# A transformer layer on one core: last filter weights on 128 rows, modulation tiles spread over four groups, first normalised inputs read from PSUM

## The chip, the core and the metric

The kernel runs on one core of a Trainium2 chip. TensorE (PE) multiplies; VectorE (DVE) and ScalarE (ACT) do the elementwise work; SyncE (SP) has a queue of its own from which it issues DMA transfers. Each engine works through its instructions in order. The metric is the device time of one execution in microseconds (us), and the median of several runs is compared.

## The reference

One layer of a backbone over 256 latent tokens with 256 context tokens, D = 1024, in float32. Every sub-layer is normalised and modulated by numbers that come from `c` (latent) or `c_ctx` (context) through one large matrix `w_ada`:

```
mod = silu(c) @ w_ada + b_ada            # 9 x 1024 numbers; the same for c_ctx
h   = rmsnorm(s, g_pre) * (1 + scale) + shift
ffn: s + 0.5 * gate * rmsnorm((silu(h @ w_gate) * (h @ w_up)) @ w_out, g_post)   # d_ff 2816
```

The layer is FFN 1, then token mixers (a long convolution and a differential attention), then FFN 2. The filter of the long convolution is made by a small MLP over 256 positions:

```
h = sin(freq * (z @ w1 + b1)); h = sin(freq * (h @ w2 + b2)); h = sin(freq * (h @ w3 + b3))
h = h @ w4                               # 256 x 64 by 64 x 2048
k = [h_fwd * decay, h_bwd * decay reversed] / (sum |k| + eps)
```

## The kernel before

**Numbers in two parts.** Matmuls have to keep float32 accuracy, so each operand is split into a high part, rounded to the type float32r, and the rest. `split` does it: ACT copies the high part, DVE subtracts. Three matmuls (`mm3`: high by high, high by low, low by high) make one product.

**Weights.** All weights of the layer come in units of 128 x 1024 (or 128 x 896) in a fixed list `plan`. `W()` hands out the next unit and has `prefetch` load and split later ones: four buffers `raw`, three of `wh` and `wl`. SP issues the loads, ACT makes `wh`, DVE makes `wl`, PE multiplies.

**FFN 1** is cut into groups over d_ff, `GROUPS1 = [(0, 7), (7, 14), (14, 22)]` in tiles of 128. Each group has a c loop, in which `ffn_in` takes two weight units and 48 matmuls (`ffi`) per tile c and `ffn_act` makes the activation `sg` and its parts `ah` and `al`, and a d loop over 8 output tiles, in which `ffn1_out` takes one unit and 3 matmuls (`ffo`) for each tile c of the group, 21 in the first two groups. These two groups work on all 512 columns (256 latent, 256 context). The third group runs twice, first on the 256 latent columns ("group 2" in the table below), then on the 256 context columns ("group 3"). The first three c of group 0 are done in the prologue, over quarters of the model's width, since the first modulation numbers arrive by quarters (`ada_quarter`, `ada_row`, `ada_cols`); so its c loop begins with c = 3. The prologue's instructions stand in program order; after it, `InOrder.pin = False` lets a scheduler choose the order on each engine.

**Modulation numbers.** The other 56 tiles of `w_ada` (128 x 1024, 512 KB each) are loaded by `ada(i)` into two buffers `adaw`, and DVE multiplies a tile by the broadcast `silu(c)` and sums it along the row (`junk`, a reduction). The first 24 tiles are needed for the context as well and take two reductions each, the others one. These reductions keep their order in the program. A table says how many tiles `some_ada` issues behind each c and each d of a group:

```
ADA = [([0] * 6 + [2], [1] * 8), ([3] * 5 + [4] * 2, [2] * 8), ([1] * 8, [0] * 8), ([0] * 8, [0] * 8)]
```

**The filter MLP** is a generator, `filters()`, which FFN 1 pumps forward between its own matmuls. Its last layer has `h3` on 128 rows (high part of the hidden values in rows 0 to 63, low part in 64 to 127) and the weights `fw4` loaded twice, in both halves of the rows. Two matmuls make a product `fo`: `h3` by `w4h` on 128 rows, and the high half of `h3` by `w4l` on 64. Eight such products are made, two at each of four places.

**The first normalised inputs.** In the prologue `tok_bcast` leaves 1/rms of each token, spread over all partitions, in a PSUM tile `bc`; ACT copies it to `rb`, and `normed(q)` multiplies two k tiles of the latent and of the context input by it on DVE, to give `xr`; `ada_cols` makes `hh` and `hl` of them.

Of the kernel before, what the change touches and what calls it, by code (L numbers as in the profile page):

```python
# [35 lines left out]
WARM, WARM2, WARM3, WARM4 = 9, 2, 5, 10  # L36
NF, NF1 = 4, 2

ADA = [([0] * 6 + [2], [1] * 8), ([3] * 5 + [4] * 2, [2] * 8), ([1] * 8, [0] * 8), ([0] * 8, [0] * 8)]


V_C, V_CC, V_NG, V_BA, V_CW, V_CB, V_HB, V_SG = 0, 8, 16, 64, 136, 208, 232, 240
# [23 lines left out]
def tile_layer(ctx: ExitStack, tc: tile.TileContext, A: dict, out: bass.AP):  # L66
# [14 lines left out]
    def G(name, dt=F32):  # L81
        return gp.tile([P, 512], dt, tag="g", bufs=NG, name=name)

    def T(name, dt=F32):
        return gp.tile([P, 512], dt, tag="t", bufs=NT, name=name)
# [133 lines left out]
    def split(src, hi, lo):  # L219
        act.activation(hi, src, AF.Copy)  # L220
        dve.tensor_tensor(lo, src, hi.bitcast(F32), ALU.subtract)
# [64 lines left out]
    def tok_bcast(y, n):  # L286

        bc = ps("bc")
        for i in range(n):
            pe.matmul(bc[:, i * P:(i + 1) * P], lhsT=y[:, i:i + 1].to_broadcast([P, P]), rhs=ident,  # L290
                             start=True, stop=True)
        return bc[:, :n * P]
# [122 lines left out]
    def filters():  # L415
        fz = T("fz")
        nc.sync.dma_start(fz[0:64, 0:448], A["fzw"])
        hcur = fz[0:64, 0:SEQ]
        fw4 = [G("fw4") for _ in range(4)]
        decay = [G("decay") for _ in range(4)]  # L420
        fh, fl = Arr("fh", 4, P, F32R), Arr("fl", 4, P, F32R)
        for i in (0, 2, 1, 3):
            for r in range(2):
                nc.sync.dma_start(fw4[i][64 * r:64 * r + 64, :], A["fw4"][:, i * 512:(i + 1) * 512])
        for i in (0, 2, 1, 3):
            nc.sync.dma_start(decay[i], A["decay"][:, i // 2, (i % 2) * 512:(i % 2) * 512 + 512])
        fraw = T("fraw")
        nc.sync.dma_start(fraw, A["dft"])
        for i in range(3):
            o = ps("fmlp")[0:64, 0:SEQ]  # L430
            pe.matmul(o, lhsT=fz[0:64, SEQ + 64 * i:SEQ + 64 * i + 64], rhs=hcur, start=True, stop=True)
            hn = T("fhid")[0:64, 0:SEQ]
            fsin(hn, o, i)
            hcur = hn
            yield

        h3 = T("h3", F32R)[:, 0:SEQ]
        act.activation(h3[0:64, :], hcur, AF.Copy)
        dve.tensor_tensor(h3[64:P, :], hcur, h3[0:64, :].bitcast(F32), ALU.subtract)
        w4 = [(G("w4h", F32R), G("w4l", F32R)[0:64, :]) for _ in range(4)]  # L440
        for i in (0, 2, 1, 3):
            act.activation(w4[i][0], fw4[i], AF.Copy)
            dve.tensor_tensor(w4[i][1], fw4[i][0:64, :], w4[i][0][0:64, :].bitcast(F32), ALU.subtract)
        yield
        yield
        for k in range(4):
            fh.at(k), fl.at(k)
        split(fraw, fh.tiles[0], fl.tiles[0])
        nrm = ps("nrm")
        pds, abl = [], []  # L450
        for cb in range(2):
            pd = []
            for tt in range(2):
                hf, hb = T("hf"), T("hb")
                for z, dst in ((0, hf), (1, hb)):
                    o = ps("fo")
                    r = slice(tt * P, (tt + 1) * P)
                    pe.matmul(o, lhsT=h3[:, r], rhs=w4[2 * z + cb][0], start=True, stop=False)
                    pe.matmul(o, lhsT=h3[0:64, r], rhs=w4[2 * z + cb][1], start=False, stop=True)
                    mk = vec[:, V_MASK:V_MASK + 1] if (z == 1 and tt == 0) else 1.0  # L460
                    dve.scalar_tensor_tensor(dst, o, mk, decay[2 * tt + cb], ALU.mult, ALU.mult)
                parts = []
                for op in (ALU.add, ALU.subtract):
                    v = T("pd")
                    dve.tensor_tensor(v, hf, hb, op)
                    vh, vl = G("ph", F32R), G("pl", F32R)
                    split(v, vh, vl)
                    parts.append((vh, vl))
                pd.append(parts)
                act.activation(hf, hf, AF.Abs)  # L470
                act.activation(hb, hb, AF.Abs)
                if tt == 0:
                    ab = T("ab")
                    dve.tensor_tensor(ab, hf, hb, ALU.add)
                else:
                    dve.tensor_tensor(ab, ab, hf, ALU.add)
                    dve.tensor_tensor(ab, ab, hb, ALU.add)
                yield
            yield
            for w in range(2):  # L480
                eo = [ps("kf") for _ in range(2)]
                for tt in range(2):
                    mm3(eo[tt], fh.at(2 * w + tt), fl.at(2 * w + tt), pd[tt][w][0], pd[tt][w][1], True, True)
                for slot, v in butterfly(w, eo, "kev"):
                    nc.sync.dma_start(kdram[:, cb, slot, :], v)
                yield
                yield
            for j in range(4):
                pe.matmul(nrm[:, cb * 4 + j:cb * 4 + j + 1], lhsT=ab[:, j * P:(j + 1) * P], rhs=ones[:, 0:1],
                          start=True, stop=True)  # L490
        dve.tensor_scalar(rn, nrm[:, 0:8], EPS, None, ALU.add)
        dve.reciprocal(rn, rn)
# [23 lines left out]
    def ada_row(q):  # L516
        n = 4
        row = T("row")
        act.activation(row[0:n, :], arow[q][0:n, :], AF.Copy)
        arow[q] = row[0:n, :]  # L520
# [18 lines left out]
        for k in range(n):  # L539
            pe.matmul(arow[q][0:4, :], lhsT=c4[:, k, :], rhs=araw[q, k], start=k == 0, stop=False)  # L540

    def normed(q):
        for k in (2 * q, 2 * q + 1):
            xr[k] = T("xr")
            dve.tensor_tensor(xr[k][:, 0:SEQ], xs[:, k, :], rb[:, 0:SEQ], ALU.mult)
            dve.tensor_tensor(xr[k][:, SEQ:T2], cs.at(k), rb[:, SEQ:T2], ALU.mult)

    def ada_cols(q):
        acol = ps("acol")
        for j in range(4):  # L550
            pe.matmul(acol[:, 2 * j:2 * j + 2], lhsT=arow[q][:, j * P:(j + 1) * P], rhs=sel[0:arow[q].shape[0], :],
                      start=True, stop=True)
        av = acol[:, 0:8].rearrange("p (i k r) -> p r i k", i=2, k=2)
        k0 = 2 * q
        m01 = modall[:, :, 0:16].rearrange("p r (i k) -> p r i k", i=2)[:, :, :, k0:k0 + 2]
        b01 = vec[:, V_BA:V_BA + 16].rearrange("p (i k) -> p i k", i=2)[:, :, k0:k0 + 2]
        g0 = vec[:, V_NG + k0:V_NG + k0 + 2]
        for r in range(2):
            dve.tensor_tensor(m01[:, r], av[:, r], b01, ALU.add)
        for r in range(2):  # L560
            dve.scalar_tensor_tensor(gsall[:, r, k0:k0 + 2], m01[:, r, 1], 1.0, g0, ALU.add, ALU.mult)
        for k in (k0, k0 + 1):
            for r in range(2):
                t = slice(r * SEQ, (r + 1) * SEQ)
                sh, gs = modall[:, r, k:k + 1], gsall[:, r, k:k + 1]
                if k == k0 and r == 1:
                    dve.tensor_scalar(hh[:, k, t], xr[k][:, t], gs, sh, ALU.mult, ALU.add)
                else:
                    act.activation(hh[:, k, t], xr[k][:, t], AF.Identity, bias=sh, scale=gs)
            for r in range(2):  # L570
                t = slice(r * SEQ, (r + 1) * SEQ)
                sh, gs = modall[:, r, k:k + 1], gsall[:, r, k:k + 1]
                dve.tensor_scalar(xr[k][:, t], xr[k][:, t], gs, sh, ALU.mult, ALU.add)
            dve.tensor_tensor(hl[:, k, :], xr[k], hh[:, k, :].bitcast(F32), ALU.subtract)
# [5 lines left out]
    for k in range(1, NF):  # L580
        pe.matmul(arow[0][0:4, :], lhsT=c4[:, k, :], rhs=araw[0, k], start=False, stop=False)
    ada_split(0, NF)
    rb = T("rb")
    act.activation(rb, tok_bcast(y, 4), AF.Copy)
    ada_quarter(0, NF)
    normed(0)
    prefetch(1, 3)
    keep_warm(WARM3)
    ada_row(0)
    ada_cols(0)  # L590
    ada_raw(1, NF1)
    pg = [ps("ffi") for _ in range(2 * NE)]
    acts = []
    for q in range(4):
        w = W("early", q, 0, ahead=2)
        if q < 3:
            ada_split(q + 1, NF1 if q == 0 else 0)
        if q < 2:
            ada_load(q + 2)
        n = 4 if q == 0 else 3  # L600
        quarter(q, pg[0:n], w, T2)
        w2 = W("early", q, 1, ahead=2)
        if q < 3:
            ada_quarter(q + 1, NF1 if q == 0 else 0)
            ada_row(q + 1)
            normed(q + 1)
        if n == 3:
            quarter(q, pg[3:4], w, T2, 3)
        else:
            quarter(q, pg[4:5], w2, T2)  # L610
        if q < 3:
            ada_cols(q + 1)
        quarter(q, pg[n + 1:], w2, T2, n - 3)
# [657 lines left out]
```

## Time and profile before

| what | value |
|---|---|
| median of three runs | 997.32 us (994.62, 997.32, 999.21) |
| profiled execution, its time | 996.32 us |
| its span on the core | 994.6 us |
| mean granted clock of PE | 0.994 of full |
| busy: PE, DVE, ACT | 978.8, 772.9, 491.2 us |
| bytes moved | 183.04 MB, mean 184 GB/s |

The profile shows one execution. "Busy" is the time in which an engine had an instruction under way. The steps between the starts of matmuls tell more than their durations, since matmuls overlap. Nearly all instructions are recorded under line 59, because a helper issues them, so they are told apart by the names of their tiles (`fo`, `ffo`, `wl`, `junk` and so on). The prologue with the first three c lasts until about 60 us, group 0 until about 165, group 1 until about 286, and the two halves of the last group run behind it, the latent one first.

### The profile page before, as it was taken

To read this page: it belongs to the slowest core of one execution; us is meant where nothing else is said; L and a number is where in the kernel's file an instruction comes from. 1 tells how busy PE (TensorE), PEld (TensorE's weight loads), DVE (VectorE), ACT (ScalarE), POOL (GpSimd) and SP (SyncE) were. 2 spreads that over 40 slices of the span, in tenths; PEclk is the share of its full clock that TensorE was granted. 3 is DMA by queue.
4 is the path that set the end of the run, shared out by engine and by line. 5 is a ranking of instruction groups with operands and counts; after the bars stand their busy time and mean duration, and the time that the engine had idled before them with its cause. 6 is when DMAs were issued, how large, how long until landed. Compare 5 with 4: busy or idle time off the path is not lost.

```text
span 994.6 us, 16285 instructions
## 1 busy us (share of the span) xinstructions
PE 978.8 (98%) x6250; PEld 873.0 (88%) x6250; DVE 772.9 (78%) x1471; ACT 491.2 (49%) x811; POOL 0.2 (0%) x4
## 2 busy tenths in 40 slices
PE   9999999999989999999999999999999999999996
PEld 6677787888779999999988899898899899999995
DVE  6886788998778778789877977867978777666666
ACT  6553434222124545566564445755675465444443
POOL 0000000000000000000000000000000000000000
PEclk9999999999989999999999999999999999999998
DMA  9845274677889755555653245444445546656661
GB/s 316 304 133 169 72 255 150 232 230 242 266 267 321 251 180 174 169 188 164 217 180 106 86 160 154 144 148 128 132 130 180 163 157 195 185 180 188 189 190 64
DMA packets 63525, 183.04 MB, mean 184 GB/s; under 512 B 6792, under 2 KB 15576, under 8 KB 63448
## 3 DMA queue, kind: packets, MB, share of 16 engines
q1 hardware_dynamic: 60856, 177.80, 56.2%
q10 hardware_dynamic: 2592, 4.20, 1.6%
q8 instruction: 49, 0.80, 0.3%
q14 instruction: 28, 0.23, 0.1%
HBM read 174.63 MB, written 3.15 MB: 179 GB/s over the span
## 4 chain that ended last, share of the span: by engine, by line
PE 81%; DMA 8%; DVE 7%; ACT 2%; issue 2%; SPq 1%; DVEq 0%; ACTq 0%
PE ffi L59 29%; PE ffo L59 8%; PE ho L59 6%; DMA adaw<-in_wadaT_dram 6%; PE pk L59 4%; PE px L59 4%; PE pva L59 3%; DVE junk L59 3%; PE pq L59 2%; PE pgd L59 2%; PE yhy L59 2%; PE pv L59 2%; PE pgh L59 2%; PE yda L59 2%; PE yo L59 2%; PE arow L59 2%
## 5 line engine op out<-in xcount | busy, mean ns | idle before, releaser
L59 ACT ACTIVATE wh<-raw 128x1024 fp32r<-128x1024 f32 (+1 forms) x250 | 259.1, 1040 | 335.5 <-issue 126.9
L59 DVE TENSOR_TENSOR wl<-raw,wh 128x1024 fp32r<-128x1024 f32 (+1 forms) x250 | 298.2, 1195 | 74.0 <-ACT wh L59 72.0
L59 PE MATMUL ffi<-hh,wl 128*128 128x258 f32 (+2 forms) x832 | 259.6, 314 | 3.8 <-DVE wl L59 3.8
L59 PE MATMUL ffi<-hh,wh 128*128 128x258 f32 (+2 forms) x832 | 260.7, 315 | 0.0
L59 PE MATMUL ffi<-hl,wh 128*128 128x258 f32 (+2 forms) x832 | 248.2, 313 | 0.0
L59 PEld LDWEIGHTS ffi<-hh,wl 128*128 128x128 f32 x832 | 160.0, 192 | 13.1 <-DVE wl L59 4.3
L59 PEld LDWEIGHTS ffi<-hh,wh 128*128 128x128 f32 x832 | 160.1, 192 | 11.7 <-issue 1.4
L59 PEld LDWEIGHTS ffi<-hl,wh 128*128 128x128 f32 x832 | 157.3, 192 | 9.0
L59 DVE CUSTOM_DVE_ANT_0 junk<-adaw,cb 128x1024 f32<-128x1024 f32 x80 | 97.7, 1221 | 26.3 <-DMA adaw<-in_wadaT_dram 25.4
L59 PE MATMUL ho<-wh,a 128*128 128x512 f32 x176 | 55.9, 390 | 0.0
L59 PE MATMUL ffo<-a,wh 128*128 128x256 f32 x256 | 46.8, 284 | 0.1
L59 PE MATMUL ffo<-al,wh 128*128 128x512 f32 x112 | 43.7, 390 | 0.4 <-DVE al L59 0.4
L59 PE MATMUL ffo<-ah,wh 128*128 128x512 f32 x112 | 43.9, 392 | 0.0
L59 PE MATMUL ffo<-ah,wl 128*128 128x512 f32 x112 | 43.6, 389 | 0.0
L59 PEld LDWEIGHTS ffo<-a,wh 128*128 128x128 f32 x256 | 40.0, 192 | 0.5 <-DVE a L59 0.5
L59 PEld LDWEIGHTS ho<-wh,a 128*128 128x128 f32 x176 | 33.1, 188 | 6.6
L59 PE MATMUL px<-hh,wh 128*128 128x256 f32 x128 | 36.2, 283 | 0.0
L59 PE MATMUL px<-hl,wh 128*128 128x256 f32 x128 | 36.2, 283 | 0.0
L59 PE MATMUL px<-hh,wl 128*128 128x256 f32 x128 | 36.2, 283 | 0.0
L59 PE MATMUL ffo<-a,wl 128*128 128x256 f32 x128 | 36.2, 283 | 0.0
L59 PE MATMUL ho<-wl,a 128*128 128x512 f32 x88 | 34.4, 390 | 0.0
L59 ACT ACTIVATE e<-sc,sm 128x512 f32<-128x512 f32 x32 | 21.8, 685 | 11.4 <-DVE sm L59 4.1
(312 smaller groups left out, 1979.6 us busy)
## 6 DMA issues: line engine op xcount, KB each, us to landing
raw<-in_wi_dram SPq DMA_DIRECT2D x100, 512.0 KB, 3.6
adaw<-in_wadaT_dram SPq DMA_DIRECT2D x56, 512.0 KB, 4.4
raw<-in_win_dram SPq DMA_DIRECT2D x56, 512.0 KB, 3.6
raw<-in_wo_dram SPq DMA_DIRECT2D x38, 512.0 KB, 3.6
araw<-in_wada_dram SPq DMA_DIRECT2D x32, 256.0 KB, 6.2
raw<-in_wo_dram SPq DMA_DIRECT2D x16, 448.0 KB, 3.7
raw<-in_winv_dram SPq DMA_DIRECT2D x8, 512.0 KB, 4.4
raw<-in_whyo_dram SPq DMA_DIRECT2D x8, 512.0 KB, 3.5
```

Of the source, the lines that this page charges most:

```text
L59: r = op(*args, **kwargs)
```

## The change

Three edits. (a) `w4l` is made on all 128 rows and multiplied with all of `h3`, so that the product of the two low parts is added as well. (b) The table `ADA`: the c loop of group 0 issues 7 tiles (2, 2, 1, 2 behind c = 3 to 6) instead of 2, the d loop of group 1 issues 8 instead of 16, the d loop of group 2 stays at none and its c loop at one per c, and two tiles stand behind the first two c of group 3. Tiles issued by the end of group 0: 15 instead of 10; of group 1: 46 instead of 49; of group 2: 54 instead of 56. (c) The first call of `normed` reads `bc` in PSUM; the copy `rb` comes behind `ada_row(0)`, and later calls read `rb`.

```
-ADA = [([0] * 6 + [2], [1] * 8), ([3] * 5 + [4] * 2, [2] * 8), ([1] * 8, [0] * 8), ([0] * 8, [0] * 8)]
+ADA = [([0] * 3 + [2, 2, 1, 2], [1] * 8), ([3] * 5 + [4] * 2, [1] * 8), ([1] * 8, [0] * 8), ([1] * 2 + [0] * 6, [0] * 8)]
...
-        w4 = [(G("w4h", F32R), G("w4l", F32R)[0:64, :]) for _ in range(4)]
+        w4 = [(G("w4h", F32R), G("w4l", F32R)) for _ in range(4)]
         for i in (0, 2, 1, 3):
-            act.activation(w4[i][0], fw4[i], AF.Copy)
-            dve.tensor_tensor(w4[i][1], fw4[i][0:64, :], w4[i][0][0:64, :].bitcast(F32), ALU.subtract)
+            split(fw4[i], *w4[i])
...
-                    pe.matmul(o, lhsT=h3[0:64, r], rhs=w4[2 * z + cb][1], start=False, stop=True)
+                    pe.matmul(o, lhsT=h3[:, r], rhs=w4[2 * z + cb][1], start=False, stop=True)
...
-    def normed(q):
+    def normed(q, rb):
...
-    rb = T("rb")
-    act.activation(rb, tok_bcast(y, 4), AF.Copy)
+    bc = tok_bcast(y, 4)
     ada_quarter(0, NF)
-    normed(0)
+    normed(0, bc)
     prefetch(1, 3)
     keep_warm(WARM3)
     ada_row(0)
+    rb = T("rb")
+    act.activation(rb, bc, AF.Copy)
...
-            normed(q + 1)
+            normed(q + 1, rb)
```

How the instructions move on an engine is seen in the order of each kernel. On DVE, in group 0's c loop, at the third sine of the filter MLP (`fa` and `fk` are its steps; `ISA junk` is a reduction, `ISA modall` its result's read-out):

```order
 L59 TENSOR_SCALAR fa<-fa 64x256
+L59 ISA junk,modall<-adaw,cb_150 128x1024
+L59 ISA modall 128x1
+L59 ISA junk,modall<-adaw,cb_151 128x1024
+L59 ISA modall 128x1
 L59 TENSOR_SCALAR fa<-fmlp,vec 64x256
-L59 TENSOR_TENSOR wl<-raw,wh 128x1024
+L59 ISA junk,modall<-adaw,cb_150 128x1024
+L59 ISA modall 128x1
 L59 TENSOR_SCALAR fk<-fa 64x256
```

Reductions that stood behind group 0's last `al` now stand among the steps of the sine; before, only a `wl` stood there. On PE, in group 0's d loop of the changed kernel, 17 `ffo` matmuls behind the loop's first (`kf` are matmuls of the filter's transform, which read the parts `ph` and `pl`):

```order
+L59 MATMUL ffo<-ah,wl 128x512
+L59 MATMUL kf<-ph,fh 128x512
+L59 MATMUL kf<-pl,fh 128x512
+L59 MATMUL kf<-ph,fl 128x512
+L59 MATMUL kf<-ph,fh 128x512
+L59 MATMUL ffo<-ah,wh 128x512
+L59 MATMUL ffo<-al,wh 128x512
+L59 MATMUL ffo<-ah,wl 128x512
+L59 MATMUL kf<-pl,fh 128x512
+L59 MATMUL kf<-ph,fl 128x512
+L59 MATMUL ffo<-ah,wh 128x512
```

The scheduler has spread these matmuls: in the kernel before, the six `kf` stood together behind the 21st `ffo`. Nine `ffo` stand between the last of these `kf` and the first matmul that reads the `al` of c = 6. On DVE, in group 1's d loop (`hsb` adds an output tile to what group 0 left):

```order
 L59 TENSOR_TENSOR hsb<-ffo,hsb 128x512
-L59 TENSOR_TENSOR wl<-raw,wh 128x896
-L59 ISA junk,modall<-adaw,cb_150 128x1024
-L59 ISA modall 128x1
-L59 ISA junk,modall<-adaw,cb_150 128x1024
-L59 ISA modall 128x1
+L59 ISA junk,modall<-adaw,cb_150 128x1024
+L59 ISA modall 128x1
+L59 TENSOR_TENSOR wl<-raw,wh 128x896
 L59 TENSOR_TENSOR hsb<-ffo,hsb 128x512
```

Between two output tiles there are two reductions before and one in the changed kernel, and the `wl` of a unit to come has changed places with the reduction beside it.

## Rows read from the trace of the kernel before

**Rows 1.** Page, part 1: busy us of each engine (share) and its instructions.

```profile
PE 978.8 (98%) x6250; PEld 873.0 (88%) x6250; DVE 772.9 (78%) x1471; ACT 491.2 (49%) x811; POOL 0.2 (0%) x4
```

**Rows 2.** Chain of waits near 295: start us, us, engine, what.

```profile
287.48 4.99 DMA adaw<-in_wadaT_dram
...
292.61 1.23 DVE junk L59
293.84 0.60 DVE hsb L59
294.44 1.14 DVE wl L59
...
295.63 4.38 PE ffi L59 x22
```

**Rows 3.** Stretches: length, busy PE, PEld, DVE, ACT, POOL; PEclk, DMA share, GB/s.

```profile
87.40:121.80 34.40, 34.40 (x144) 26.42 (x144) 25.30 (x40) 17.59 (x28) 0.00 (x0) 1.00 0.24 68
165.00:282.00 117.00, 116.56 (x518) 96.24 (x517) 97.03 (x146) 31.71 (x39) 0.00 (x0) 1.00 0.75 240
284.00:300.00 16.00, 12.16 (x73) 11.74 (x73) 11.89 (x18) 3.12 (x4) 0.00 (x0) 0.79 0.83 272
300.00:316.00 16.00, 16.00 (x135) 15.94 (x134) 14.31 (x30) 7.88 (x12) 0.00 (x0) 1.00 0.89 314
365.00:400.00 35.00, 35.00 (x295) 35.00 (x294) 28.92 (x57) 18.06 (x32) 0.00 (x0) 1.00 0.57 179
```

**Rows 4.** PE's timeline, 248 to 296: start, us, instruction [idle before <-releaser].

```profile
248.86 0.45 PE L59 MATMUL ffo<-ah,wh 128*128 128x512 f32 x1
249.75 0.50 PE L59 MATMUL ffo<-al,wh 128*128 128x512 f32 x1 [0.44 <-DVE al L59]
250.09 0.40 PE L59 MATMUL ffo<-ah,wl 128*128 128x512 f32 x1
...
289.24 0.51 PE L59 MATMUL ffi<-hh,wl 128*128 128x256 f32 x1 [2.10 <-DVE wl L59]
...
295.63 0.38 PE L59 MATMUL ffi<-hh,wl 128*128 128x256 f32 x1 [1.75 <-DVE wl L59]
```

**Rows 5.** SP's timeline, group 1's d loop: DMA issues.

```profile
257.18 2.24 SPq L622 DMA_DIRECT2D adaw<-in_wadaT_dram  x2
...
291.80 2.39 SPq L622 DMA_DIRECT2D adaw<-in_wadaT_dram  x2
```

**Rows 6.** PE's timeline, start of group 0's d loop.

```profile
119.80 0.39 PE L59 MATMUL ffo<-ah,wh 128*128 128x512 f32 x1
...
124.33 0.39 PE L59 MATMUL ffo<-ah,wl 128*128 128x512 f32 x1
```

**Rows 7.** PE's timeline, the last of the four `fo` places.

```profile
153.72 0.39 PE L59 MATMUL fo<-w4h,h 128*128 128x512 f32 x1
154.04 0.50 PE L59 MATMUL fo<-w4l,h 64*128 64x512 f32 x1
154.47 0.49 PE L59 MATMUL fo<-w4h,h 128*128 128x512 f32 x1
...
155.66 0.39 PE L59 MATMUL ffo<-al,wh 128*128 128x512 f32 x1
```

**Rows 8.** DVE's groups, 60 to 165: count | busy us, mean ns | idle.

```profile
L59 DVE TENSOR_TENSOR w4l<-fw,w4h 64x512 fp32r<-64x512 f32 x4 | 2.5, 676 | 0.0
```

**Rows 9.** DVE's timeline in group 0.

```profile
92.72 0.28 DVE L59 TENSOR_SCALAR fa<-fa 64x256 f32<-64x256 f32 x1
...
122.42 1.22 DVE L59 CUSTOM_DVE_ANT_0 junk<-adaw,cb 128x1024 f32<-128x1024 f32 x1
...
123.68 1.23 DVE L59 CUSTOM_DVE_ANT_0 junk<-adaw,cb 128x1024 f32<-128x1024 f32 x1
```

**Rows 10.** DVE's timeline in the prologue.

```profile
18.47 0.42 DVE L59 TENSOR_TENSOR xr<-xs,rb 128x256 f32<-128x256 f32 x1
...
21.70 0.23 DVE L59 TENSOR_TENSOR modall<-acol,vec 128x4 f32<-128x4 f32 x2 [0.68 <-PE acol L59]
```

## The prediction

> **What bounds the kernel now.** The page's busy times come first [rows 1]: PE is busy for 978.8 us of a span of 994.6, so time can only come from the few microseconds in which PE stands, and from matmuls that take longer than their columns need. The chain of waits is PE work almost everywhere, but just ahead of 295.63 it runs through the modulation tiles: an `adaw` transfer, a reduction `junk`, the addition `hsb`, the subtraction `wl`, and only then PE [rows 2]. So DVE and its transfers end last in one short stretch.
>
> The stretches [rows 3] place it. In 87.4 to 121.8 PE never stands and DVE is busy for 25.30 of 34.40 us: 9.1 us are free. In 165 to 282 (group 1) DVE is busy for 97.03 of 117 us and PE for all but 0.44. In 284 to 300 PE issues 73 matmuls at a mean granted clock of 0.79; in the next 16 us it issues 135 at full clock, with more bytes moved (314 GB/s against 272). PE's own rows [rows 4] name the waits: 0.44 us on `al` at 249.75, 2.10 on `wl` at 289.24, 1.75 on `wl` at 295.63. SP's rows [rows 5] say why `wl` is late: the pair of `adaw` issues of one output tile d stands at 257.18 and the pair six tiles later at 291.80, 5.77 us per d. PE needs 21 matmuls of 512 columns per d: at 0.227 us each (119.80 to 124.33 are 20 steps [rows 6]) that is 4.77. Each d moves two `adaw` and one `raw` of 448 KB, 1.507 MB, which in 5.77 us is 261 GB/s. The loop loses 1.0 us per d, has used up its lead by its end, and PE pays at the start of group 2.
>
> **The change, part by part.**
>
> (a) *The last filter weights on 128 rows.* The loops over `cb`, `tt` and `z` make 8 `fo` pairs, two pairs together in each of four places. In such a place 128-row and 64-row matmuls alternate, and 153.72 to 155.66 takes 1.94 us for five steps [rows 7]. Five steps at 0.227 are 1.14. The slow ones are every step that leaves or enters a 64-row matmul (0.43 from the row at 154.04 to the next), not the 64-row ones alone. With all of them on 128 rows nothing alternates, so I take the full 0.80 per place: 4 x 0.80 = **-3.2 us** on PE, which is the path there. The other bound is 0 (an `fo` step stays as long whatever its rows). The four subtractions `w4l` become 128x512 instead of 64x512, which took 676 ns [rows 8], as long as a 128x512 operation, whose step in the chain is 0.60 us [rows 2]; so this is 0. A rule speaks against it: the Trainium skill, "TensorEngine Tiling (Array Packing)", section "Theoretical Speedup", gives small contractions, 64 rows and fewer, up to a twofold gain when tiles run side by side, so fewer rows would be the cheaper form; by that (a) would be worth 0 and the sum would lose its 3.2 us. The same page's "Key Properties" says that switching mode needs a drain; by that rule the trace agrees, since the 128-row matmul behind a 64-row one is slow as well, 0.43 us.
>
> (b) *The modulation tiles.* Double reductions (the first 24 tiles) stay 24, and total reductions stay 80; they move.
>
> Group 1's d loop goes from two tiles per d to one: 0.983 MB per 4.77 us, 206 GB/s, which is below the 261 that it has reached with a reduction and transfer always waiting. So it no longer loses its lead, and the stalls at 289.24 and 295.63 go. What they cost is not their 3.85 us of idle time: 135 - 73 = 62 matmuls fewer, at 16/135 = 0.1185 us, are **-7.35 us**; the other 3.5 us are matmuls at half clock behind the two stalls (a mean granted clock of 0.79 over 16 us is 0.21 x 16 = 3.4 us of clock withheld). The stall at 249.75 goes too, since group 1's c loop has 9 double tiles instead of 14, 5 reductions fewer: 248.86 to 250.09 took 1.23 us for two steps of 0.227, **-0.78 us**. What is late next: group 2's c loop now has 8 tiles for 7, 1.573 MB per 48 x 0.1185 = 5.69 us of PE, 276 GB/s, below the 314 that 300 to 316 shows without a stall. Taken as 0; the other end is rival 2.
>
> Group 0's c loop is where the price is: five tiles more, ten reductions. One takes 1.26 us from start to start (122.42 to 123.68 [rows 9]), so 12.6 us go into a stretch with 9.1 free, and work behind them on DVE becomes late by up to 3.5. I walked DVE's queue in its new order with these steps (0.60 for 128x512 and 1.14 for a `wl` [rows 2], 1.26 a reduction). The third sine, whose last DVE operation ended at 93.0 (92.72 + 0.28), ends near 97.3, the last `w4l` at 104.1; PE wants it at 105.5, so 1.4 us are left. After six more reductions the last `al` of group 0 (c = 6) ends near 126.7, against 122.42 before. PE begins the d loop at 119.80 less the 1.6 that the first two `fo` places give back, 118.2; the new order lets 18 `ffo`, four `kf`, three `ffo`, two `kf` and nine more go ahead of the first matmul that reads that `al`: 36 x 0.227 = 8.2, so PE is there at 126.4. A stall of about 0.4, with a slower matmul behind as at 249.75: **+0.5 us**. Its bounds are 0 and, if DVE comes 2 us later than walked, 2 us of stall and one fall of the clock: 3.5 us over two stalls is 1.75 each, so 3.75. The transfers don't set this: the first two tiles lie in their buffers, and the next come while DVE is on the sine.
>
> Group 3 gets two single reductions, 2.5 us, into 365 to 400, where DVE is busy for 28.92 of 35: hidden, since 6.1 are free (without that cover, up to 1).
>
> (c) *The first normalised inputs from PSUM.* DVE's `xr` at 18.47 has no idle time ahead of it: DVE comes to it straight from other work, so it cannot begin earlier when the copy `rb` is out of its way. Further on DVE is idle for 0.68 us ahead of 21.70, where it waits for PE's `acol` [rows 10], so even an earlier end would go into that wait. Value 0. No row shows this operation with a PSUM source; if each of the four took twice its 0.42 us, 1.7 us more less the 0.68 idle would be +1.0, the other end. `rb` itself is then next read for the second pair of inputs, a quarter of the prologue later.
>
> The sum: -3.2 - 7.35 - 0.78 + 0.5 = -10.8, span 994.6 to 983.8. The profiled execution took 996.32, 1.7 over its span; that gives 985.5. The median of the runs, 997.32, is 1.0 above that execution, half of which I allow: **986.0 us**, 1.1% less. Its own range is 984 to 988.5.
>
> **The rivals.**
> 1. *Group 0 overloads DVE.* For it: ten reductions in 9.1 free us, and margins of 1.4 at `w4l` and -0.4 at the last `al`. Against it: PE has 36 matmuls ahead of that `al`. It decides from about 1 us more delay than walked. It takes 3.75 instead of 0.5: 989.2 (988.5 to 992).
> 2. *The transfers bound group 2.* If its c loop gets the 261 GB/s of group 1's d loop instead of 276, a c takes 6.03 us instead of 5.69: 8 x 0.34 = 2.7, plus a clock fall of 1.75: 990.5. Against it: 314 GB/s at 300 to 316.
> 3. *The `fo` steps stay as they are*, that is, part (a) doesn't do what it says. 3.2 less gain: 989. Against it: the slow 128-row step. (The page's rule on small contractions, above, would make this case.)
> 4. *The stall only moves*: DVE, and not the transfers, was the limit of group 1, and the reductions that remain hold PE up as before. Only 3 us are won at most: 994, within 0.5%. Against it: the chain goes through the `adaw` transfer, and DVE waits for it.
> 5. *Slower: group 0's d loop closes on itself.* There an `adaw` waits for a buffer that two reductions free, and the `raw` behind it in SP's queue waits too. If a transfer (4.99 us in the chain [rows 2]), two reductions (2.5) and some 0.5 for the turn followed each other, a d would take 8 us instead of 4.77: 8 x 3.2 = 26, less two units of lead (9.5), 16 us: 1002. It decides where a d exceeds about 7.3 us. Against it: two buffers overlap the landing with the reductions, and the loop had this load before without a PE stall.
>
> **How the numbers follow.** Chances: the forecast 0.60, rival 1 0.17, rival 2 0.07, rival 3 0.06, rival 4 0.06, rival 5 0.04. The range runs from 983.0 (no group 0 stall and none of the 1.0 offset, less 2 for the spread of the medians) to 992.0, which takes in rivals 1 to 3. Half a per cent, 5.0 us, is about what a measurement of this kernel can tell from no change: faster means below 992.3. Faster 0.60 + 0.17 + 0.07 + 0.06 less 0.04 for their upper ends: 0.86; same 0.10; slower 0.04.
>
> **What would show it.** Right: five `fo` steps in about 1.14 us; no wait on `wl` in 280 to 300, a granted clock of 1.00 there and about 135 matmuls per 16 us from group 2's start; `adaw` issues of group 1's d loop 4.8 us apart; at most one short wait on `al` or `pl` in 118 to 130. Wrong: a wait on `w4l`, `al` or `wl` over 1 us in 95 to 165 (rival 1 or 5), waits on `wl` in group 2 (rival 2), `fo` steps of 0.43 (rival 3), or the wait of 2 us still at the start of group 2 (rival 4).

## The result and the profile after

The changed kernel takes 986.5 us (median of 4 runs, 984.79 to 989.07) against 997.2 before (4 runs): a ratio of 0.9896, with a 95% interval of 0.9862 to 0.9930. The forecast was 986.0. Five more runs of the same kernel, beside 17 of the kernel before, gave 985.77 and a ratio of 0.9886 (0.9864 to 0.9908). The profiled execution took 984.79 us, its span is 983.0.

The page's first part answers to [rows 1]: PE's busy time falls by 9.4 us, DVE's and ACT's stay within 1.2 us.

```profile
PE 969.4 (99%) x6250; PEld 868.4 (88%) x6250; DVE 773.2 (79%) x1471; ACT 490.0 (50%) x811; POOL 0.2 (0%) x4
```

PE's longest waits over the whole span, with their total time, number and longest. The waits on `wl` and on `al` of [rows 4] are gone. The first line is new, and lies in the first 13 us:

```profile
PE arow L59 <- ACT sq L59: 2.7, 1, 2.7
PE warm L59 <- DVE c L59: 1.0, 1, 1.0
PE xT L59 <- DVE xtok L59: 0.8, 1, 0.8
PE yda L59 <- ACT odh L59: 0.6, 1, 0.6
```

The first `fo` place, in PE's timeline (start, us, instruction). All row counts are 128, and four steps take 0.91 us, 0.227 each, where [rows 7] had 0.32 and 0.43:

```profile
106.00 0.39 PE L59 MATMUL fo<-w4h,h 128*128 128x512 f32 x1
106.23 0.39 PE L59 MATMUL fo<-w4l,h 128*128 128x512 f32 x1
106.45 0.39 PE L59 MATMUL fo<-w4h,h 128*128 128x512 f32 x1
106.68 0.39 PE L59 MATMUL fo<-w4l,h 128*128 128x512 f32 x1
106.91 0.39 PE L59 MATMUL ffi<-hh,wh 128*128 128x512 f32 x1
```

Stretches of the changed kernel (columns as in [rows 3]). In the first, DVE is busy for 32.30 us where it was for 25.30, and PE still never stands. The second is the start of group 2, which answers to 284 to 300 of before: 135 matmuls instead of 73, clock 1.00 instead of 0.79. The last is group 3 with its two tiles, 30.80 us of DVE in 35, and no loss:

```profile
87.40:121.80 34.40, 34.40 (x152) 27.95 (x151) 32.30 (x54) 14.72 (x23) 0.00 (x0) 1.00 0.48 135
...
280.40:296.40 16.00, 16.00 (x135) 16.00 (x134) 12.61 (x23) 7.70 (x11) 0.00 (x0) 1.00 0.78 244
...
355.00:390.00 35.00, 35.00 (x294) 35.00 (x294) 30.80 (x63) 18.73 (x32) 0.00 (x0) 1.00 0.59 177
```

SP's last `adaw` issues in group 1's d loop are now 4.75 us apart, one per d and at PE's pace, against 5.77 per pair in [rows 5] (the issues ahead of them, from 246 to 270, are 2 to 4 us apart):

```profile
272.89 0.33 SPq L622 DMA_DIRECT2D adaw<-in_wadaT_dram  x1
...
277.65 0.33 SPq L622 DMA_DIRECT2D adaw<-in_wadaT_dram  x1
...
282.40 0.33 SPq L622 DMA_DIRECT2D adaw<-in_wadaT_dram  x1
```

A place in the program can be followed through two traces by the start of the first matmul there. This table is worked out from PE's timelines; the last column says what each stretch won or lost (group 1 ends at 283.70 in the kernel before, a little sooner than the 286 given at the start):

| start of | before | after | difference | change since the line above |
|---|---|---|---|---|
| first `arow` | 11.96 | 12.45 | +0.48 | |
| first `fo` | 105.50 | 106.00 | +0.50 | 0 |
| group 0's d loop | 119.80 | 118.69 | -1.10 | -1.60, two `fo` places |
| group 1 | 166.31 | 163.79 | -2.52 | -1.42, two `fo` places and +0.17 |
| group 2 | 283.70 | 280.35 | -3.35 | -0.83, wait on `al` |
| group 2's d loop | 337.40 | 326.42 | -10.98 | -7.63, waits on `wl` and clock |
| last matmul | 986.39 | 974.87 | -11.52 | -0.54 in small pieces; 0.12 longer in the second profile of the changed kernel |

### The profile page after: what moved, and what is told of

The parts are those of the page before. It is cut to its first block, busy times and chain, and to the rows that moved or that the text cites. A ratio compares the mean times of both kernels' runs of the same rounds, so it can differ in the third digit from the quotient of the medians.

```text
span 983.0 us, 16283 instructions
## 1 busy us (share of the span) xinstructions
PE 969.4 (99%) x6250; PEld 868.4 (88%) x6250; DVE 773.2 (79%) x1471; ACT 490.0 (50%) x811; POOL 0.2 (0%) x4
## 4 chain that ended last, share of the span: by engine, by line
PE 97%; DVE 1%; DMA 1%; ACT 1%; SPq 0%; issue 0%; DVEq 0%
PE ffi L59 38%; PE ffo L59 12%; PE ho L59 6%; PE px L59 5%; PE pk L59 4%; PE pva L59 4%; PE pq L59 2%; PE pgd L59 2%; PE yhy L59 2%; PE pv L59 2%; PE pgh L59 2%; PE yo L59 2%; PE yda L59 2%; PE arow L59 2%; PE sc L59 1%; PE po L59 1%
## 5 line engine op out<-in xcount | busy, mean ns | idle before, releaser
L59 ACT ACTIVATE e<-sc,sm 128x512 f32<-128x512 f32 x32 | 21.7, 683 | 11.4 <-DVE sm L59 4.2
```

What stands on the lines that cost most here:

```text
L59: r = op(*args, **kwargs)
```

## The experiments

What each gave, against the kernel before on the same chip. The last three columns, in us, are worked out from the table's places as there, without what the first 24 us differ by; a negative number is won. Where there is one run, only its trace is used:

| kernel | runs | median us | ratio (95%) | span us | up to group 1 | to group 2 | to its d loop |
|---|---|---|---|---|---|---|---|
| filter only | 10 | 994.55 | 0.9971 (0.9951 to 0.9991) | 994.9 | -3.20 | -0.50 | +0.38 |
| table only | 5 | 989.05 | 0.9919 (0.9892 to 0.9947) | 987.0 | +0.04 | -0.84 | -7.62 |
| PSUM only | 10 | 998.65 | 0.9999 (0.9976 to 1.0022) | 998.4 | +0.02 | +0.64 | +1.26 |
| `fo` on 64 rows | 1 | 992.99 | | 991.2 | -1.50 | -0.83 | -1.23 |
| half the loads | 1 | 988.0 | | 985.9 | 0 | -0.84 | -7.62 |
| half the reductions | 1 | 998.18 | | 996.3 | +0.03 | -0.48 | -0.81 |
| three buffers | 6 | 989.63 | 0.9933 (0.9912 to 0.9955) | 987.8 | +0.02 | -0.84 | -7.62 |
| heavy group 0 | 1 | 990.2 | | 988.4 | +1.22 | -0.04 | -7.63 |
| light group 0 | 12 | 992.83 | 0.9948 (0.9932 to 0.9964) | 990.8 | -3.21 | -0.84 | -7.62 |
| full again | 5 | 985.77 | 0.9886 (0.9864 to 0.9908) | 983.9 | -3.03 | -0.84 | -7.62 |
| full, three buffers | 5 | 985.67 | 0.9887 (0.9863 to 0.9912) | 985.3 | -3.00 | -0.84 | -7.62 |
| full, more warming | 4 | 985.14 | 0.9878 (0.9855 to 0.9901) | 984.4 | -3.03 | -0.83 | -7.63 |

**The three parts alone.** The diff of the change, cut to one part each.

> Only part (a), w4l on 128 rows. My theory (alternating row counts cost the steps): five steps of each fo place in 1.14 us, so PE is 3.0 us earlier from the last place on (group 1 starts 3.0 earlier); the waits on wl at the start of group 2 stay, and since the adaw transfers of group 1's d loop set their own pace there, they may grow by part of the 3.0. Span 991.5 to 993.5 against 994.6. Rival (the steps shrank in the full change because the scheduler put other work there): fo steps of 0.43 stay and nothing moves at group 1's start.

> Only part (b), the table. My theory: the fo places stay at 1.94 us, the waits on al (0.44) and on wl (2.10 and 1.75) go, PE is some 8.4 us earlier by 302, span 986.2 (985.5 to 987.5). Rival 1 (group 0 overloads DVE): the last al of group 0 or the filter's last weights hold PE up by 1 us or more in 95 to 130, span above 988.

> Only part (c), the first normalised inputs from PSUM. My theory: nothing, the first ffi matmul starts as long behind the first arow matmul as before (11.45 us) within 0.1, span 994.6 within 1. Rival: the reads of PSUM are slower or the later copy rb is missed, and that distance grows by up to 1.0.

By the ratios the times move by -2.9 us (0.29%), -8.1 (0.81%) and 0, together -11.0, and the full change by -10.4 to -11.4: the parts add up, as far as intervals of 2.0 to 3.4 us to either side can say. The stretches say it closer: -3.20 of the filter and -0.84 - 7.62 of the table, against -3.00 to -3.03, -0.84 and -7.62 in the full change. The filter alone wins 3.20 us by group 1's start and keeps the waits on `wl`; its profiled span, 994.9, was outside what was expected, because its first 24 us took 3.9 longer than before's (see the last section). The table alone has no wait in group 0 and wins 0.84 and 7.62. In the profile of the PSUM part the first `ffi` stands 13.14 us behind the first `arow`, not within 0.1 of 11.45 as expected, but the difference lies ahead of the ninth `arow`, before this part's multiplications, where the granted clock was 0.70 (13 to 17 us); from the ninth `arow` to the first `ffi` it is 5.93 us in both kernels. The multiplication that reads PSUM takes 0.42 us, as long as the one that reads `rb` in [rows 10]; in the changed kernel, DVE's timeline:

```profile
18.96 0.42 DVE L59 TENSOR_TENSOR xr<-xs,bc 128x256 f32<-128x256 f32 x1
```

The two later columns of the PSUM part are the old waits, which differ from profile to profile: in the last column +1.26 here, and +0.38, -1.23 and -0.81 in the other kernels that still have them. From group 2's start to its d loop those four and the kernel before take 52.47 to 54.96 us, and every kernel without the waits takes 46.07. So what their removal is worth depends on the execution it is measured against: 6.4 to 8.9 us, and 7.63 against the profile shown here.

**What slows the filter's matmuls.** The high matmul of each product on the high part's 64 rows too:

```
-                    pe.matmul(o, lhsT=h3[:, r], rhs=w4[2 * z + cb][0], start=True, stop=False)
+                    pe.matmul(o, lhsT=h3[0:64, r], rhs=w4[2 * z + cb][0][0:64, :], start=True, stop=False)
```

> The kernel before, with both matmuls of each fo product on the 64 rows of the high part (the product of h's low part with w4's high part is left out). Theory that the switch between row counts costs: within a place nothing alternates, only its entry and exit switch, and five steps take about 1.5 us instead of 1.94. Rival, 64-row matmuls are slow in themselves: every fo step stays at 0.43 or becomes so, 1.94 us or more.

The last `fo` place of this kernel, PE's timeline:

```profile
152.48 0.39 PE L59 MATMUL ffo<-ah,wl 128*128 128x512 f32 x1
152.80 0.49 PE L59 MATMUL fo<-w4h,h 64*128 64x512 f32 x1
153.14 0.39 PE L59 MATMUL fo<-w4l,h 64*128 64x512 f32 x1
153.37 0.39 PE L59 MATMUL fo<-w4h,h 64*128 64x512 f32 x1
153.60 0.39 PE L59 MATMUL fo<-w4l,h 64*128 64x512 f32 x1
153.93 0.50 PE L59 MATMUL ffo<-ah,wh 128*128 128x512 f32 x1
154.27 0.40 PE L59 MATMUL ffo<-al,wh 128*128 128x512 f32 x1
```

From 152.80 to 154.27 five steps take 1.47 us. Among themselves the 64-row matmuls step at 0.23, like those of 128 rows; the entry costs 0.32 and 0.34, the exit 0.33 and 0.34. So a switch costs 0.2 us, spread over the steps on both sides of it, and neither row count is slow in itself. The kernel before has four switches in a place, 0.80 us.

**What ends last in group 1's d loop.** Two kernels halve one thing each. Half the loads: `some_ada` hands the second tile of a d the buffer of the first.

```
             w = ada(i, w if share else None)
...
-            some_ada(ADA[gi][1][d])
+            some_ada(ADA[gi][1][d], gi == 1)
```

> The kernel before, but in group 1's d loop the two tiles of a d are reduced from one transfer: 0.983 MB per d, reductions as before (those modulation numbers are wrong). Theory that the adaw transfers end last: the waits on wl at the start of group 2 (2.10 and 1.75 us) go, span about 987. Rival, DVE's reductions are the limit there: the waits stay within 0.5 us, span 994 to 995.

Half the reductions: the first of the two tiles is read over 16 columns only.

```
-                dve_late.tensor_tensor_reduce(junk, w, cb2[r], 1.0, ...
+                dve_late.tensor_tensor_reduce(junk[:, :n], w[:, :n], cb2[r][:, :n], 1.0, ...
...
             ada(i, 16 if short and i == nada else D)
```

> The kernel before, but in group 1's d loop the first of the two tiles of a d is reduced over 16 columns only: transfers as before, half the reduction time (that modulation number is wrong). If bytes per second are the limit, 261 GB/s: the waits on wl stay, span 993 to 995. If DVE's busy time is the limit, they go, span about 987. If the two buffers are (landing and reductions taking turns), they go or shrink to less than half as well, span 987 to 990, and the half-load kernel loses them too.

And a third buffer, with all work left in: `tag="adaw", bufs=3`.

> The kernel before with three adaw buffers instead of two, nothing else. If the limit of group 1's d loop is that landing and reductions take turns in two buffers: transfers start earlier, more than 300 GB/s in that loop, the waits on wl go, span about 987. If bytes per second are the limit (261 GB/s): the d loop keeps its 5.77 us per pair of tiles, at most one buffer of lead (2 us) is won, span 991 to 994.6.

Half the loads removes both waits on `wl`. Half the reductions leaves them, 4.2 us in all (PE's waits, first line):

```profile
PE ffi L59 <- DVE wl L59: 4.2, 3, 1.9
```

So the transfers end last, as the prediction said, and DVE's busy time doesn't (22.2 us in 245 to 284 here, 28.3 in the kernel before). The chain of waits of the kernel before shows the loop at work: a transfer starts when a reduction has freed its buffer, and the next reduction starts when a transfer has landed.

```profile
251.95 1.23 DVE junk L59
253.21 4.49 DMA adaw<-in_wadaT_dram
...
257.83 1.23 DVE junk L59
259.10 4.65 DMA adaw<-in_wadaT_dram
...
263.88 1.23 DVE junk L59
```

In the changed kernel the same stretch of the chain is PE's work alone:

```profile
187.86 54.57 PE ffi L59 x240
242.43 38.08 PE ffo L59 x168
```

But 261 GB/s was no ceiling. With three buffers the same loop, and the stretch behind it, move more (266 and 272 GB/s in the kernel before):

```profile
245.00:284.00 39.00, 39.00 (x176) 32.34 (x175) 34.15 (x51) 8.92 (x10) 0.00 (x0) 1.00 0.87 303
284.00:300.00 16.00, 16.00 (x135) 16.00 (x135) 13.47 (x26) 7.25 (x11) 0.00 (x0) 1.00 0.94 351
```

So bytes per second were not the limit, and what held the loop, as far as these kernels show, was how many tiles can be on their way at once: one more buffer wins the same 0.84 and 7.62 us as the new table does, and its expectation for a limit in bytes (at most 2 us of lead) is refuted. One result doesn't fit yet. If landing and reductions take turns, half the reductions was expected to shrink the waits to less than half, and it didn't. Its transfers took longer instead: in the chain behind each short reduction they land in 4.75 to 5.86 us, where the kernel before has 4.29 to 4.99, and the pairs stay 5.6 us apart against 5.77. Why they landed later is not shown.

**The price in group 0.** Four tiles more there, taken from groups 2 and 3; and the opposite, group 0 as before and its five tiles in group 3:

```
-ADA = [([0] * 3 + [2, 2, 1, 2], [1] * 8), ([3] * 5 + [4] * 2, [1] * 8), ([1] * 8, [0] * 8), ([1] * 2 + [0] * 6, [0] * 8)]
+ADA = [([0] * 3 + [3, 3, 2, 3], [1] * 8), ([3] * 5 + [4] * 2, [1] * 8), ([1] * 6 + [0] * 2, [0] * 8), ([0] * 8, [0] * 8)]   # heavy
+ADA = [([0] * 6 + [2], [1] * 8), ([3] * 5 + [4] * 2, [1] * 8), ([1] * 8, [0] * 8), ([1] * 7 + [0], [0] * 8)]               # light
```

> The changed kernel with four more tiles in group 0's c loop (3, 3, 2, 3 behind c = 3 to 6), taken from group 2's c loop and from group 3. Eight reductions more, 10 us, in a stretch whose free time is used up: the last w4l and the last al of group 0 come 2.5 to 7.5 us later than in the changed kernel, PE stands 6 to 9 us in 100 to 140 and its clock falls, span 989 to 994 against 983.0. If PE's matmuls ahead still cover it, as in the changed kernel: below 985.

> The changed kernel without the five tiles more in group 0's c loop; they go behind c = 0 to 6 of group 3, and one double tile of group 1's c loop counts twice more often again (14 double tiles). Theory that group 0 hides its ten reductions and that the five double tiles held up al at the end of group 1's c loop: no gain in group 0 (fo to the d loop's end as in the changed kernel within 0.2), the wait on al near 245 is back (0.8 us), and group 3's seven reductions (8.8 us in 6.1 free) cost 0 to 2.7; span 983.5 to 986.5. Rival (group 0's load costs PE time in the changed kernel): the d loop of group 0 ends 0.5 us or more earlier, span below 982.5.

In the heavy kernel PE stands in group 0's d loop, 2.15 us here (PE's timeline) and 1.5 us on a `wl` at 162:

```profile
125.08 0.50 PE L59 MATMUL kf<-ph,fh 128*128 128x512 f32 x1 [2.15 <-ACT ph L59]
```

That is 3.65 us of idle time, where 6 to 9 were expected, and the clock, expected to fall, stays at 1.00 (118 to 167). The loss is larger than the idle time, since steps beside the waits are slow too (0.29 to 0.53 us): by the start of group 1 it is at +1.22, where the filter alone gives -3.20, and another 0.79 is lost in group 1's c loop, 5.2 us together. So rival 1's mechanism is real, and 4 tiles beyond this table set it off.

The light kernel wins 3.21 up to group 1, the changed table with the new filter 3.00 to 3.03 in four profiles: the five tiles cost 0.2 us, as expected. Its other two expectations missed. The wait on `al` is not back (see the next section). And its seven tiles in group 3 cost more than 2.7 us: PE waits there for the last sum of squares, the granted clock falls to 0.50 behind it, and 4.5 us are lost between its c loop's start and its d loop's (PE's timeline):

```profile
394.00 0.71 PE L59 MATMUL st<-ones,acc 128*128 128x1 f32 x4 [3.01 <-DVE acc L59]
```

**Whether anything is left to win.**

> The changed kernel itself once more, as the reference of this call. Span 983 when PE's clock stays up in the first 25 us, 986 to 987 when it falls there; median 985 to 988, ratio to the kernel before 0.987 to 0.992.

> The changed kernel with a third adaw buffer. If the changed table has already removed every wait on the adaw transfers: same as the changed kernel within 1 us. If earlier transfers collide with the weights' in group 0: slower by 1 to 3 us, with waits on wl in 60 to 165.

```
-WARM, WARM2, WARM3, WARM4 = 9, 2, 5, 10
+WARM, WARM2, WARM3, WARM4 = 9, 10, 5, 10
```

> The changed kernel with 10 instead of 2 idle-time matmuls ahead of the first arow matmul (1.8 us of PE work in a wait of 1.6 to 2.8 us). If the spread of the executions comes from PE's clock falling behind that wait (3 us in three of ten profiles): no fall in any execution, all within 1.5 us of each other, median 1 to 2 us below the changed kernel. If the spread comes from elsewhere (a later stretch): the same spread, and up to 1.5 us slower where the wait is short.

The third buffer adds nothing to the new table: both remove the same waits. (Its profiled span is 2.3 us above the changed kernel's, not within 1 us as expected; its first `ffi` stands 1.4 us later, so 1.4 of that lie in the first 24 us.) The warming matmuls gave four executions between 984.72 and 986.21, against 984.37 to 987.82 for five of the changed kernel beside it. That points the expected way, but the medians are 0.6 apart, not 1 to 2 as expected, and can't be told apart; no version is shown to beat the changed kernel.

## Why the prediction was right, point by point

- **The filter, -3.2.** Measured -3.20 in the filter's kernel and -3.21 in the light one. The mechanism, alternation and not 64 rows, is shown by the 64-row kernel. So rival 3 falls. With it falls, for this kernel, what the Trainium skill's "Theoretical Speedup" (in "TensorEngine Tiling (Array Packing)") would have made of the part: without tiles side by side a 64-row matmul steps at 0.23 like one of 128 rows. With the Trainium skill's "Key Properties" (in "TensorEngine Tiling (Array Packing)"), a drain at each change of mode, the runs agree in that each switch costs 0.2 us; that it is a drain no row shows.
- **The waits on `wl`, -7.35.** Measured -7.63. That idle time and half clock together make it, and not the 3.85 us of idle alone, is borne out by the table's kernel, the three buffers and the half loads, all at -7.62. That the size is met to 0.3 us is partly luck: both numbers rest on one profile of the kernel before, and others would have given 6.4 to 8.9. The step "below the 261 that it has reached" was right in its result, but 261 was what two buffers gave, not the memory; 303 GB/s went through with three. And that DVE and its transfers end last "in one short stretch" was misread: the chain of waits of the kernel before runs through them from 164.94 to 295.58, all of group 1.
- **The wait on `al`, -0.78.** The size was right (-0.83) by luck, and the reason is not borne out. I gave it to five fewer double tiles in group 1's c loop. The light kernel has all 14 of them and loses the wait too; so does the kernel with half the loads, which is the kernel before in all that precedes. DVE's rows show what it hangs on: the last `al` stands behind two reductions that wait for `adaw`. In the kernel before:

```profile
244.17 1.23 DVE L59 CUSTOM_DVE_ANT_0 junk<-adaw,cb 128x1024 f32<-128x1024 f32 x1 [2.17 <-DMA adaw<-in_wadaT_dram]
...
246.26 1.23 DVE L59 CUSTOM_DVE_ANT_0 junk<-adaw,cb 128x1024 f32<-128x1024 f32 x1 [0.85 <-DMA adaw<-in_wadaT_dram]
...
249.01 0.68 DVE L59 TENSOR_TENSOR al<-sg,ah 128x512 fp32r<-128x512 f32 x1
```

  and in the kernel with half the loads, in the same order and 1.4 to 1.8 us sooner:

```profile
242.82 1.22 DVE L59 CUSTOM_DVE_ANT_0 junk<-adaw,cb 128x1024 f32<-128x1024 f32 x1 [1.16 <-DMA adaw<-in_wadaT_dram]
...
244.44 1.23 DVE L59 CUSTOM_DVE_ANT_0 junk<-adaw,cb 128x1024 f32<-128x1024 f32 x1 [0.39 <-DMA adaw<-in_wadaT_dram]
...
247.19 0.68 DVE L59 TENSOR_TENSOR al<-sg,ah 128x512 fp32r<-128x512 f32 x1
```

  So this wait is the landing of `adaw` again, close enough to its limit that one profile has it and another not. DVE has the same order up to this `al` in seven kernels, and counted from the start of group 1's d loop the `al` ends at 4.91 us (before), 4.45 (filter), 5.56 (PSUM), 2.93 (64 rows), 2.87 (half the loads), 4.43 (half the reductions) and 3.47 (light). Only before and PSUM have a wait on it; up to 3.47 us it costs nothing. With the new table it ends at 2.70 in all five profiles. So the new table removes the wait, but what that is worth against another execution of the kernel before is anything from 0 to 1.5 us. What makes the tiles land sooner in one profile than in another was not tried.
- **Group 0, +0.5.** Measured +0.17, and at another place than forecast. The walk through DVE's queue held: the third sine ended at 97.66 (walked 97.3), the last `w4l` at 104.66 (104.1), the last `al` at 126.74 (126.7):

```profile
97.38 0.28 DVE L59 TENSOR_SCALAR fa<-fa 64x256 f32<-64x256 f32 x1
...
102.77 1.89 DVE L59 TENSOR_TENSOR w4l<-fw,w4h 128x512 fp32r<-128x512 f32 x3
...
126.05 0.69 DVE L59 TENSOR_TENSOR al<-sg,ah 128x512 fp32r<-128x512 f32 x1
```

  PE needs that `al` 36 matmuls behind 118.69, at 127.00, 0.26 us after it was there: the forecast stall of 0.4 did not come. The first 12 us had taken 0.5 longer than in the kernel before, which moves DVE and PE alike (the margin is 0.26 to 0.29 in all four profiles with this table and filter). Counted with it, PE came as walked and DVE 0.5 us sooner. The cost lies at `pl`, the low part that a `kf` matmul reads: DVE ends it at 124.33, PE's weight load for that matmul waits 0.3 us for it, and the matmul's step is 0.34 instead of 0.227 (the load's wait, 118 to 130, then PE's timeline):

```profile
PEld kf L59 <- DVE pl L59: 0.3, 1, 0.3
```

```profile
124.39 0.50 PE L59 MATMUL kf<-pl,fh 128*128 128x512 f32 x1
124.73 0.39 PE L59 MATMUL kf<-ph,fl 128*128 128x512 f32 x1
```

  That wait stands in all four profiles, and neither in the light kernel nor in the table's alone, whose two slow `fo` places bring PE 1.6 us later. It is 0.11 of the 0.17 us; the rest lies in steps about 0.01 longer. The term was mis-sized by 0.3.
- **Group 3 and group 2, 0.** Right: no wait in either. The light kernel shows that group 3 was hidden for two tiles and would not have been for seven.
- **The inputs from PSUM, 0.** Right, by the third kernel alone: 0.9999 (0.9976 to 1.0022), and by the 0.42 us of its multiplications; the other end, +1.0 for reads at half the speed, falls. DVE's wait for `acol` behind them is 0.69 us in the changed kernel, as the 0.68 of [rows 10].
- **Rivals 4 and 5.** No wait moved into group 1, and into group 0's d loop none but the 0.3 us of a weight load on `pl`; half the reductions leaving the waits speaks against rival 4 directly.

## What to carry to other kernels

Price a stall by the matmuls that are missing in its stretch, since the matmuls behind it at half clock cost as much again as the wait (3.85 us idle, 7.63 lost). When a prefetched stream ends last, count what is in flight before counting bytes: one more buffer won here what moving eight tiles elsewhere did. And a walk through an in-order engine's queue with steps from the trace was good to 0.6 us over 40 us, enough to see that a load just fits; four tiles more did not, at 5.2 us. Before a saving is compared with a forecast to a few tenths, look at how far the old wait itself varies: over five profiles it did by 2.5 us.

## What the runs showed that was not expected

The first 24 us, though the same program in the kernel before and in the filter's, differ by 3.9 us between their profiles, more than the filter's whole gain. In the profile of the filter's kernel PE waits 2.54 us ahead of its first `arow`, and the granted clock of the next 4 us is 0.50, the lower of its two levels; the first rows are PE's timeline there:

```profile
9.43 0.61 PE L59 MATMUL warm<-ones 128*128 128x128 f32 x4
12.58 1.72 PE L59 MATMUL arow<-araw,c 128*4 128x512 f32 x2 [2.54 <-ACT sq L59]
```

and the stretch from 13 to 17 us:

```profile
13.00:17.00 4.00, 4.00 (x12) 2.00 (x11) 1.12 (x7) 3.59 (x7) 0.00 (x0) 0.50 0.98 346
```

The changed kernel's profile has a wait of 2.69 us at the same place and a clock of 1.00 behind it, and half the reductions has 1.7 us and 0.51, so the length of the wait alone doesn't decide. What does was not settled.
